# Decoder block on one Trainium2 core: the feed-forwards' output parts added to H by an accumulating transfer

## The chip, the cores and the metric

The kernel runs on one core of one Trainium2 chip. The core has a matrix engine (TensorE, PE in the profile; PEld is its weight load), VectorE (DVE), ScalarE (ACT), GpSimd (POOL), a queue engine (SyncE, SP) that issues transfers, and 16 DMA engines that carry them. Each engine works through its own instructions in the order in which the program gave them; an instruction that waits holds up everything behind it on its engine. The metric is the device time of one execution in microseconds. Before the change two runs gave 990.43 and 991.58 us, a median of 991.0 us.

## What is computed

One decoder block on 512 tokens of width 1024, in float32. Two SwiGLU feed-forwards stand around a token mixer, each with its own normalisation, shift, scale and gate; the modulation comes from a condition vector `c`.

```python
def swiglu(u, w_in, w_out):
    a, b = jnp.split(u @ w_in, 2, axis=-1)
    return (jax.nn.silu(a) * b) @ w_out
...
        u = modulate(rmsnorm(h, g_norm_ffn1[l]), sh1, sc1)
        h = h + 0.5 * gt1 * swiglu(u, w_ffn1_in[l], w_ffn1_out[l])
        u = modulate(rmsnorm(h, g_norm_mix[l]), sh2, sc2)
        h = h + gt2 * token_mixing(u, cos, sin, w_in[l], w_pool[l], pool_scale[l],
                                   w_pool_branch[l], w_attn_branch[l], w_out[l])
        u = modulate(rmsnorm(h, g_norm_ffn2[l]), sh3, sc3)
        h = h + 0.5 * gt3 * swiglu(u, w_ffn2_in[l], w_ffn2_out[l])
    return rmsnorm(h, g_final)
```

The hidden width of each feed-forward is 2816. The change touches the two lines `h = h + 0.5 * gt * swiglu(...)`, and of them only how the sum over the hidden width is added to `h`.

## The kernel before

**Layout.** Everything is held feature-major: `H` is eight tiles `H[0]` to `H[7]` of 128 features by 512 tokens in float32, 256 KB each, and stays in on-chip memory throughout. Every product is done in three matmuls (`mm3`, lines 360 to 362): the weights and the activations are each split into a high and a low part of a shorter format, and high times high, high times low and low times high are summed in one bank of the matrix engine's accumulator memory. There are eight banks of 128 x 512; the feed-forwards go round six of them (`nb`).

**Weights.** They arrive from main memory in chunks, mostly 512 KB (128 x 1024), by transfers of the SP queue (`fetch`, line 245). `split_hi` (ScalarE, line 317) copies a chunk into the ring `whi`, and `split_lo` (VectorE, line 329) subtracts to get `wlo`. `look(4)` makes sure that the splits of the next four chunks are in the program ahead of the matmuls that come now. Some chunks are not loaded as such but made by VectorE from two others (`make`, line 261), as the products of the hidden layer are done in a seven-product scheme in place of eight.

**One feed-forward.** The 22 tiles of the hidden width are made in pairs: the first few by `ffn_pair`, the others by `duo`, which runs seven `product`s of 24 matmuls of 256 columns each (lines 745 to 747) into three banks A, B and C. After product 0, ScalarE copies A to C; product 2 goes on adding to A, and so cannot begin before that copy is done. The output product is cut into five parts of the hidden width, `PARTS = ((0, 4), (4, 8), (8, 12), (12, 16), (16, 22))`. As soon as four hidden tiles are ready, a part runs: for each of the eight output tiles `m`, two by two, 12 matmuls of 512 columns into a bank, and then line 900, one VectorE instruction that multiplies the bank by the gate and adds it to `H[m]`. In the first pair of a part the matmuls of the two banks are interleaved. The first four parts go this way, in both feed-forwards: 2 x 4 x 8 = 64 instructions of line 900. The fifth part has another code (line 933 and `out_tail` or `out_end`), since the next normalisation starts beside it, and is not touched. Between two parts lie more pairs of the hidden layer, so each of the first four parts is followed by at least one `duo`.

**What else runs there.** In the first feed-forward VectorE also multiplies the modulation weights (`bg`, `ada_do`, line 387): a 512 KB row block of `w_ada`, loaded by SP into `cs`, `AR` or another buffer, once for each output tile in parts 1 to 3. Actions that a `duo` puts off (`later`) come at `step()`.

**Order.** The tile framework is told to keep the program's order on each engine (`manual_schedule`) and puts in the semaphores: an instruction that writes a tile waits for the last reader of what lay there before. A tile of a pool with `bufs=1`, such as those of `fw`, has one place, and each new tile of the same name takes it again.

Of the kernel before, what the change touches and what calls it, by code (L numbers as in the profile page):

```python
# [8 lines left out]
F32 = mybir.dt.float32  # L9
F32R = mybir.dt.float32r  # L10
I32 = mybir.dt.int32
AF = mybir.ActivationFunctionType
OP = mybir.AluOpType

P = 128
T = 512
# [117 lines left out]
def pairs_before(n, part):  # L134

    k1 = PARTS[part][1]
    return k1 if part + 1 == len(PARTS) or (n == 2 and part == 0) else k1 + 2
# [9 lines left out]
class Kernel:  # L147
# [6 lines left out]
    def plan(self):  # L154
# [38 lines left out]
        def ffn(n, ins, outs, first):  # L193
# [4 lines left out]
            for part, (k0, k1) in enumerate(PARTS):  # L198
# [9 lines left out]
                plain(outs[part * KT // 2:(part + 1) * KT // 2] if part + 1 < len(PARTS) else outs[-KT:])  # L208

        ffn(0, f1i, f1o, FIRST)  # L210
        shift(4)
        base = len(self.order)
# [5 lines left out]
        self.shifted.update(range(base, base + 4))  # L218
        shift(3)
        ffn(2, f2i, f2o, 0)  # L220
        shift(5)
        self.fetched = self.done = self.made = 0
# [638 lines left out]
    def ffn(self, n, j, last=None):  # L861

        nc, v = self.nc, self.nc.vector
        gate = self.mod[:, 24 * n + 16:24 * n + 24]

        def beside():
            if n == 0:
                self.bg()
                if part == 0:
                    self.bg()  # L870

        for part, (k0, k1) in enumerate(PARTS):
            tail = part + 1 == len(PARTS)
            extra = 1
            while j < pairs_before(n, part):
                if j < PLAIN[n]:
                    self.ffn_pair(j, beside)
                    j += 1
                else:
                    self.duo(n, j, last, tail and j + 2 == FT, extra)  # L880
                    last, extra = None, 0
                    j += 2
            if n == 0:
                last = self.beside_out(part) or last
            nk = k1 - k0
            hk = [(self.HH[k % NH], self.HL[k % NH]) for k in range(k0, k1)]
            if not tail:
                for m in range(0, KT, 2):
                    self.look(4)
                    w = self.take()  # L890
                    bs = [self.nb(), self.nb()]

                    for ka, kb in ((0, nk - 1), (nk - 1, nk)) if m == 0 else ():
                        for i in range(2):
                            for k in range(ka, kb):
                                self.mm3(bs[i], *w[nk * i + k], *hk[k], k == 0, k == nk - 1)
                    for i, b in enumerate(bs):
                        for k in range(nk if m else 0):
                            self.mm3(b, *w[nk * i + k], *hk[k], k == 0, k == nk - 1)
                        v.scalar_tensor_tensor(self.H[m + i], b, gate[:, m + i:m + i + 1], self.H[m + i],  # L900
                                               op0=OP.mult, op1=OP.add)

                        if n == 0 and part:
                            self.later((6, 13)[i], self.bg) if m + 2 == KT else self.bg()
                        if self.todo:
                            self.todo.pop(0)()
                    self.step()
                continue

            def ks(m):  # L910
                w = self.take()
                self.split_hi()
                return [(hi, lo, *hk[k]) for k, (hi, lo) in enumerate(w)]

            self.look()
            if n == 2:
                self.sums.close()
                op = self.f2.enter_context(self.tc.tile_pool(name="f2o", bufs=1))
                self.OO = op.tile([P, KT * T], F32, name="out").rearrange("p (m t) -> p m t", m=KT)
                self.O = [self.OO[:, m, :] for m in range(KT)]  # L920

            kl = [ks(0), ks(1)]
            bs = [self.nb(), self.nb()]
            for ka, kb in ((0, nk - 2), (nk - 2, nk)):
                for m in range(2):
                    for k in range(ka, kb):
                        self.mm3(bs[m], *kl[m][k], k == 0, k == nk - 1)
            for m in range(3 if n else 4):
                if m > 1:
                    bs.append(self.nb())  # L930
                    for k, x in enumerate(ks(m)):
                        self.mm3(bs[m], *x, k == 0, k == nk - 1)
                v.scalar_tensor_tensor(self.H[m], bs[m], gate[:, m:m + 1], self.H[m], op0=OP.mult, op1=OP.add)
                add = self.sumsq(m, self.H[m])
                if n == 2:
                    nc.scalar.activation(self.O[m], self.H[m], AF.Copy, scale=self.g(3)[:, m:m + 1])
                self.split_lo()
                add()
                if m:
                    self.split(self.done)  # L940
                self.fetch()
            if n:
                self.out_end((3, 4, 5, 6, 7), ks, gate)
            else:
                self.out_tail((4, 5, 6, 7), ks, gate, 1, lambda m: self.X[0][:, m % 2 * HT:])
# [849 lines left out]
```

## Time and profile before

| | |
|---|---|
| time of the two runs, us | 990.43 and 991.58, median 991.0 |
| span of the profiled execution, us | 988.9 |
| median of the runs less this span, us | 2.1 |
| mean granted TensorE clock | 0.999 |
| HBM read, written | 135.29 MB, 2.24 MB |
| first and last start of line 900, us from the start of the span | 92.8 and 908.1 |
| first and last start of line 933 (fifth parts), us | 327.7 and 958.5 |

The page has no time of the profiled execution besides its span, which runs from the first to the last instruction; the 2.1 us are what lies around it. Busy times are shares of that span. Matmuls overlap one another in the records (one is listed with 0.39 us although the next starts 0.23 us later), so the time of a row of matmuls is read from starts. Idle time of an engine that holds nobody up costs nothing.

### The profile page before, as it was taken

How to read it: one execution, taken by the hardware profiler on the slowest of the kernel's cores; microseconds unless marked ns; L12 is line 12 of the kernel's file. 1: busy time of each engine (PE TensorE's matmuls, PEld its weight loads, DVE VectorE, ACT ScalarE, POOL GpSimd, SP SyncE). 2: the span in 40 equal slices, each digit the busy share in tenths (PEclk: the TensorE clock that was granted, in tenths of full speed). 3: DMA queues.
4: the chain of work that ended last, by engine and by line, in shares of the span. 5: the costliest groups of instructions: out<-in, count | busy, mean ns of one | idle time of the engine just before them, and what ended most of it. 6: DMA issues, size and time to landing. Idle time of an engine off the chain costs nothing.

```text
span 988.9 us, 16359 instructions
## 1 busy us (share of the span) xinstructions
PE 980.7 (99%) x6688; PEld 893.3 (90%) x6688; DVE 784.3 (79%) x1090; ACT 474.7 (48%) x712; POOL 29.7 (3%) x31
## 2 busy tenths in 40 slices
PE   9999999999999999999999999999999999999997
PEld 7888999989999899888879998998899898998997
DVE  7989979889797777887878877868787776676764
ACT  5453643625435453445545552455355254352553
POOL 0000000000000000007200000000000000000002
PEclk9999999999999999999999999999999999999999
DMA  9856446465563426664233326513344134241312
GB/s 353 276 196 224 150 149 187 156 196 165 183 199 109 137 57 201 223 192 153 72 122 108 107 81 218 171 44 104 98 155 133 46 117 138 86 150 44 106 44 86
DMA packets 44876, 141.74 MB, mean 143 GB/s; under 512 B 6273, under 2 KB 9089, under 8 KB 44802
## 3 DMA queue, kind: packets, MB, share of 16 engines
q1 hardware_dynamic: 44224, 140.18, 43.9%
q8 instruction: 52, 0.85, 0.4%
q10 hardware_dynamic: 578, 0.53, 0.2%
q14 instruction: 22, 0.18, 0.1%
HBM read 135.29 MB, written 2.24 MB: 139 GB/s over the span
## 4 chain that ended last, share of the span: by engine, by line
PE 94%; DVE 2%; ACT 1%; SPq 1%; issue 1%; POOL 0%; DMA 0%; POOLq 0%; ACTq 0%; DVEq 0%
PE bank L360 15%; PE bank L361 15%; PE bank L362 15%; PE bank L746 13%; PE bank L745 13%; PE bank L747 13%; PE bank L1721 2%; PE bank L1723 1%; PE bank L1725 1%; SPq L1053 1%; PE bank L1397 1%; PE bank L1099 1%; PE bank L1150 1%; PE bank L1398 1%; PE bank L1399 1%
## 5 line engine op out<-in xcount | busy, mean ns | idle before, releaser
L329 DVE TENSOR_TENSOR wlo<-raw,whi 128x1024 fp32r<-128x1024 f32 (+4 forms) x162 | 170.6, 1066 | 52.2 <-ACT whi L317 51.9
L745 PE MATMUL bank<-UH,whi 128*128 128x256 f32 x640 | 176.7, 276 | 0.0
L746 PE MATMUL bank<-UL,whi 128*128 128x256 f32 x640 | 176.7, 276 | 0.0
L747 PE MATMUL bank<-UH,wlo 128*128 128x256 f32 x640 | 176.7, 276 | 0.0
L317 ACT ACTIVATE whi<-raw 128x1024 fp32r<-128x1024 f32 (+4 forms) x162 | 146.3, 920 | 58.4 <-DVE raw L261 55.0
L360 PE MATMUL bank<-HI,whi 128*128 128x512 f32 (+1 forms) x406 | 146.2, 360 | 0.0
L361 PE MATMUL bank<-HK,whi 128*128 128x512 f32 (+1 forms) x406 | 145.9, 359 | 0.0
L362 PE MATMUL bank<-HI,wlo 128*128 128x512 f32 (+1 forms) x406 | 145.8, 359 | 0.0
L329 DVE TENSOR_TENSOR wlo<-X,whi 128x1024 fp32r<-128x1024 f32 (+3 forms) x104 | 112.0, 1084 | 31.2 <-ACT whi L317 30.9
L745 PEld LDWEIGHTS bank<-UH,whi 128*128 128x128 f32 x640 | 120.1, 188 | 0.4
L746 PEld LDWEIGHTS bank<-UL,whi 128*128 128x128 f32 x640 | 120.2, 188 | 0.0
L747 PEld LDWEIGHTS bank<-UH,wlo 128*128 128x128 f32 x640 | 120.1, 188 | 0.0
L745 PE MATMUL bank<-SH,whi 128*128 128x256 f32 x408 | 112.7, 276 | 0.0
L746 PE MATMUL bank<-SL,whi 128*128 128x256 f32 x408 | 112.6, 276 | 0.0
L747 PE MATMUL bank<-SH,wlo 128*128 128x256 f32 x408 | 112.6, 276 | 0.0
L317 ACT ACTIVATE whi<-X 128x1024 fp32r<-128x1024 f32 (+3 forms) x104 | 95.7, 943 | 34.1 <-DVE X L261 33.4
L360 PE MATMUL bank<-UH,whi 128*128 128x512 f32 (+1 forms) x304 | 105.9, 348 | 0.0
L361 PE MATMUL bank<-UL,whi 128*128 128x512 f32 (+1 forms) x304 | 104.5, 344 | 0.1
L362 PE MATMUL bank<-UH,wlo 128*128 128x512 f32 (+1 forms) x304 | 104.2, 343 | 0.0
L362 PEld LDWEIGHTS bank<-HI,wlo 128*128 128x128 f32 x406 | 76.2, 188 | 11.7
L360 PEld LDWEIGHTS bank<-HI,whi 128*128 128x128 f32 x406 | 76.2, 188 | 11.5
L361 PEld LDWEIGHTS bank<-HK,whi 128*128 128x128 f32 x406 | 76.3, 188 | 11.3
(345 smaller groups left out, 1838.0 us busy)
## 6 DMA issues: line engine op xcount, KB each, us to landing
raw<-wmix SPq DMA_DIRECT2D x44, 512.0 KB, 3.8
raw<-wf1i SPq DMA_DIRECT2D x31, 512.0 KB, 4.7
raw<-wf2i SPq DMA_DIRECT2D x30, 512.0 KB, 3.7
ada<-wada SPq DMA_DIRECT2D x23, 512.0 KB, 5.6
AR<-wada SPq DMA_DIRECT2D x19, 512.0 KB, 4.5
X<-wf2i SPq DMA_DIRECT2D x14, 512.0 KB, 3.8
cs<-wada SPq DMA_DIRECT2D x12, 512.0 KB, 3.7
X<-wf1i SPq DMA_DIRECT2D x12, 512.0 KB, 4.3
```

Of the source, the lines that this page charges most:

```text
L317: self.nc.scalar.activation(self.hi[:, y], r[:, x], AF.Copy)
L329: self.nc.vector.tensor_tensor(self.lo[:, y], r[:, x], self.hi[:, y], op=OP.subtract)
L360: M(ps, hi, uh, start=start, stop=False)
L361: M(ps, hi, ul, start=False, stop=False)
L362: M(ps, lo, uh, start=False, stop=stop)
L745: M(o, hi, uh, start=start and p == 0 and k == 0, stop=False, skip_group_check=True)
L746: M(o, hi, ul, start=False, stop=False, skip_group_check=True)
L747: M(o, lo, uh, start=False, stop=k == 3, skip_group_check=True)
L1053: nc.sync.dma_start(w[32 * o:32 * o + 32], t[32 * i:32 * i + 32])
L1099: nc.tensor.matmul(S[:, o], q[:, toks], k[:, ks], start=True, stop=True, skip_group_check=True)
L1150: self.nc.tensor.matmul(self.bO[64 * h:64 * h + 64, P * hp:P * hp + P], x, pt[:, (2 * h + j) * P:(2 * h + j + 1) * P], start=j == first, s ...
L1721: M(b, hi, self.UH[k], start=k == 0, stop=False)
```

## The change

In the first four output parts of both feed-forwards, the VectorE instruction of line 900 is gone. In its place ScalarE copies the bank, times the gate (one number for each of the 128 partitions), to a tile `add0` or `add1`, for the even and the odd output tile of a pair; and a transfer that GpSimd issues reads this tile and adds it to `H[m]` where `H[m]` lies. Both tiles belong to the pool `fw`, which has one place for each name, so the copy for output tile `m + 2` waits until the transfer of output tile `m` is over. `fw` grows by these two tiles of 2 KB in each partition, and the pools that are opened after it lie 4 KB further on.

```diff
-                        v.scalar_tensor_tensor(self.H[m + i], b, gate[:, m + i:m + i + 1], self.H[m + i],
-                                               op0=OP.mult, op1=OP.add)
+                        t = self.fw.tile([P, T], F32, name=f"add{i}")
+                        nc.scalar.activation(t, b, AF.Copy, scale=gate[:, m + i:m + i + 1])
+                        nc.gpsimd.dma_start(self.H[m + i], t, accum_op=OP.add)
```

## The prediction

> **What bounds the kernel now.** I read the page first: the busy times, the chain of work that ended last, and the DMA queues.
>
> ```profile
> span 988.9 us, 16359 instructions
> PE 980.7 (99%) x6688; PEld 893.3 (90%) x6688; DVE 784.3 (79%) x1090; ACT 474.7 (48%) x712; POOL 29.7 (3%) x31
> ...
> q1 hardware_dynamic: 44224, 140.18, 43.9%
> ...
> PE 94%; DVE 2%; ACT 1%; SPq 1%; issue 1%; POOL 0%; DMA 0%; POOLq 0%; ACTq 0%; DVEq 0%
> ```
>
> The matrix engine is idle for 988.9 - 980.7 = 8.2 us in all, and 94% of the chain is its own work. VectorE, which the change relieves, has 2% of the chain. Next, the busy times by stretch, for the output parts that line 900 belongs to (three of the eight, and the sum over all eight; columns: length, PE, PEld, DVE, ACT, POOL with their counts, granted clock, DMA share, GB/s).
>
> ```profile
> 80.50:102.30 21.80, 21.80 (x97) 18.02 (x97) 20.48 (x28) 9.19 (x12) 0.00 (x0) 1.00 0.58 199
> ...
> 201.80:223.60 21.80, 21.80 (x102) 18.22 (x101) 19.16 (x31) 4.64 (x5) 0.00 (x0) 1.00 0.55 175
> ...
> 827.00:849.00 22.00, 22.00 (x103) 18.40 (x102) 15.20 (x19) 6.01 (x7) 0.00 (x0) 1.00 0.14 47
> ...
> sum 175.20, PE 175.20 PEld 146.69 DVE 138.82 ACT 48.41 POOL 0.00; mean PE 21.90 PEld 18.34 DVE 17.35 ACT 6.05 POOL 0.00
> ```
>
> PE is busy for 175.20 of 175.20 us: where the change acts there is no idle matrix time to win. So the question is only whether the new route holds the matmuls up. Last, the timeline of one part and the start of the `duo` behind it, on three engines.
>
> ```profile
> 826.08 0.40 PE L360 MATMUL bank<-HI,whi 128*128 128x512 f32 x1
> ...
> 847.87 0.27 PE L366 MATMUL bank<-UH,whi 128*128 128x240 f32 x1
> 847.98 0.28 PE L745 MATMUL bank<-UH,whi 128*128 128x256 f32 x1
> ...
> 850.71 0.28 PE L745 MATMUL bank<-SH,whi 128*128 128x256 f32 x1
> ```
>
> ```profile
> 831.07 1.43 DVE L900 SCALAR_TENSOR_TENSOR H<-bank,mod,H 128x512 f32<-128x512 f32 x2 [1.98 <-PE bank L362]
> ...
> 837.19 0.75 DVE L900 SCALAR_TENSOR_TENSOR H<-bank,mod,H 128x512 f32<-128x512 f32 x1 [0.56 <-PE bank L362]
> ...
> 842.63 0.75 DVE L900 SCALAR_TENSOR_TENSOR H<-bank,mod,H 128x512 f32<-128x512 f32 x1 [1.76 <-PE bank L362]
> ...
> 848.07 0.75 DVE L900 SCALAR_TENSOR_TENSOR H<-bank,mod,H 128x512 f32<-128x512 f32 x1 [1.76 <-PE bank L362]
> ```
>
> ```profile
> 850.91 0.58 ACT L752 ACTIVATE bank<-bank 128x512 f32<-128x512 f32 x1 [5.22 <-PE bank L747]
> 851.40 1.05 ACT L317 ACTIVATE whi<-raw 128x1024 fp32r<-128x1024 f32 x1
> ```
>
> A part's 96 matmuls take 847.87 - 826.08 = 21.79 us without a hole, a bank of 12 is ready every 2.72 us, a pair every 5.44 us (837.19, 842.63, 848.07). Line 900 waits for PE each time, nobody for it. Product 0 of the `duo` starts at 847.98, product 1 at 850.71, so product 2 at 850.71 + 2.73 = 853.44; it needs ScalarE's copy of A to C, which runs 850.91 to 851.49. That is the first deadline that ScalarE meets behind a part.
>
> **What is taken off VectorE.** The costs of both routes, from the groups of instructions:
>
> ```profile
> L900 DVE SCALAR_TENSOR_TENSOR H<-bank,mod,H 128x512 f32<-128x512 f32 x64 | 47.2, 749 | 28.1 <-PE bank L362 28.1
> L1050 ACT ACTIVATE rt<-bank,cst 128x512 f32<-128x512 f32 x4 | 2.8, 689 | 5.7 <-PE bank L362 5.7
> L745 PE MATMUL bank<-UH,whi 128*128 128x256 f32 x640 | 176.7, 276 | 0.0
> L745 PE MATMUL bank<-SH,whi 128*128 128x256 f32 x408 | 112.7, 276 | 0.0
> ```
>
> 64 x 0.749 us, 47.2 us with the overlaps, and 28.1 us of waits ahead of them leave VectorE. It lets the splits and `make`s behind them start earlier, and on the path that is worth nothing, because PE waits for none of them: 0 us.
>
> **What is put on ScalarE.** 64 copies from a bank with a factor for each partition. Line 1050 is the same shape and form: 0.69 us. A part has eight, 5.5 us; ScalarE has 4.6 to 9.2 us of work in the 21.8 us, so it stays below 15. As work this is hidden. What can hurt is the order: a copy that waits holds the splits and `duo` copies behind it. It waits for two things. The bank, as line 900 did: the splits behind it then come no earlier than the pair that is being multiplied, and they are four chunks ahead of need, one chunk a pair, so 0. And the place of its tile, held until the transfer of two output tiles earlier is over.
>
> **The tile's turn.** Call c the time from one copy's start to the end of its transfer. The copy of tile m1 starts at 837.19 - 5.44 = 831.75 in that part. Three turns later comes m7, so it starts at the later of 848.07 and 831.75 + 3c; the even tiles start 0.7 us earlier with the same c, and give the same bound. Behind m7 stand 0.69 us of itself, one split (1.05) and the copy of A to C (0.58), to be over at 853.44. So m7 may start up to 851.12, and c up to (851.12 - 831.75) / 3 = 6.46 us costs nothing. Beyond it PE stands 3c - 19.4 us in a part, 24c - 155 us in eight. Banks come round after three pairs and are no tighter.
>
> The trace has no transfer issued by GpSimd and none that adds. The nearest rows (DMA issues with KB and median us to landing; then SP's issue times, ns least, median, most):
>
> ```profile
> k<-wada SPq DMA_DIRECT2D x6, 512.0 KB, 6.3
> ...
> rt<-tr SPq DMA_DIRECT2D x16, 64.0 KB, 2.0
> ...
> out_dram<-out SPq DMA_DIRECT2D x4, 256.0 KB, 2.2
> tr<-wmix SPq DMA_DIRECT2D x3, 256.0 KB, 4.0
> ```
>
> ```profile
> L245 SPq DMA_DIRECT2D X<-wf2i x14: 327/328/672, 692.7 to 910.0; - x14
> ...
> L1053 SPq DMA_DIRECT2D rt<-tr x16: 512/582/590, 398.3 to 440.8; - x16
> ```
>
> Least: 0.33 us issue and 2.2 us landing, c = 0.69 + 0.33 + 2.2 = 3.2. Most: 0.58 and 6.3 (512 KB among other loads, since the addition reads 256 KB from each of two places), c = 7.6. I take 0.58 and 4.0, the 256 KB load that came down among others: c = 5.3. Then m2, due only 3.4 us after m0, waits 1.9 us and m6 some 1.6 us; m7 starts on time. Cost 0; at the upper end (24 x 7.6) - 155 = 27 us.
>
> **What is put on the DMA engines.** 64 x 262,144 bytes = 16.8 MB, or 33.6 MB if the read of H counts as much. At q1's rate (43.9% for 140.18 MB) that is 5 to 11% more. It is tightest in the first feed-forward: 175 GB/s at a share of 0.55 makes 318 GB/s at full share, and a part's 2.1 MB or 4.2 MB need 6.6 or 13.2 us of 21.8: 0.85, or 1.16 and 3.4 us of backlog. That delays a weight load or a `w_ada` load for VectorE, which after the change has 21.8 - (19.16 - 6.0) = 8.6 us free there; the splits are two to four chunks (5 us and more) ahead. Cost 0; without that cover 3.4 x 4 = 14 us.
>
> **What is put on GpSimd.** Its busy time in the parts is 0.00, so no work of it is delayed; it waits for each copy, with only the next addition behind it. H is next read late:
>
> ```profile
> L933 DVE SCALAR_TENSOR_TENSOR H<-bank,mod,H x7: 745/750/751, 327.7 to 958.5; 128x512 f32<-128x512 f32 x7
> ```
>
> Line 933 first runs at 327.7, two `duo`s behind the fourth part. The 4 KB by which later pools move: the matmul is 276 ns from UH as from SH, which lie apart, so 0.
>
> **One rule against the change.** GpSimd's work beside VectorE is seen in the mixer:
>
> ```profile
> 440.90 1.22 DVE L329 TENSOR_TENSOR wlo<-raw,whi 128x1024 fp32r<-128x1024 f32 x1
> ...
> 452.17 2.08 DVE L329 TENSOR_TENSOR wlo<-raw,whi 128x1024 fp32r<-128x1024 f32 x1
> ```
>
> ```profile
> 451.27 1.90 POOL L1223 TENSOR_TENSOR rt<-tr 128x527 f32<-128x527 f32 x1 [8.03 <-ACT tr L1217]
> ```
>
> The same subtraction takes 0.86 us longer beside a GpSimd addition. If each of 64 issues did this, VectorE would lose 55 us, against 47 us taken off: still no wait of PE. The Trainium skill ("SBUF — State Buffer", Who interferes with whom) says that an instruction of VectorE with two inputs in this memory contends with a GpSimd instruction that reads it, which the two rows bear out, and not with one that only writes; by it the writing of descriptors would cost VectorE nothing, and the sum is the same. Its box on VectorE keeping GpSimd from writing descriptors is the third rival below.
>
> **The rivals.** First, *the tile's turn is too long* (slower): c above 6.46, from the issue or from a landing like the 6.3 us row. At c = 7.6 it is 991 + 27 = 1018 us; 2% (20 us) begins at c = 7.3. For it: the 512 KB rows and a doubled read; against it: the 2.0 and 2.2 us of on-chip reads, and a DMA share of 0.14 in the second feed-forward. Second, *the addition goes piece by piece* (slower): if the 256 KB landed as four 64 KB rows one after the other, 4 x 2.0, c = 0.69 + 0.58 + 8.0 = 9.3, and 24 x 9.3 - 155 = 68 us: 1059. No row speaks for or against it. Third, *VectorE holds GpSimd up* (slower): were each issue to wait for two of VectorE's 1.22 us instructions, c = 5.3 + 2.4 = 7.7 and the time 991 + 30 = 1021. VectorE is busy 15 to 20 of 22 us there, which is for it; 8 issues in 21.8 us leave room, which is against it. The Trainium skill ("SBUF — State Buffer", SBUF: two separate sides) gives that blocking for modes in which VectorE uses both port pairs, and names copies; nearly all instructions in these parts have two tensors, so it should be rare here. Fourth, *VectorE's share of the chain shrinks* (faster): 2 us of the 8.2 us of idle PE, 989; the chain's VectorE pieces lie at the ends of stages, where line 900 isn't. Fifth, *it does not do what it says*, VectorE still waiting for the additions before its next use of H: that use is two `duo`s later, so 991 again.
>
> **How the numbers follow.** 988.9 span, 2.1 around it by the median, 0 of change: 991. Chances: forecast 0.57, tile's turn 0.21, piece by piece 0.09, VectorE holds GpSimd 0.07, faster 0.04, fifth 0.02. Below 988 lies at most 0.02. Above: 0.09 of the second rival and perhaps 0.08 of the first and third beyond 1030 (24 x 8.1 - 155 = 39 us); the range 988 to 1030 so holds about 0.8. The forecast case alone is 988 to 996. About 2% is what a measurement can tell from no change. Slower by more: 0.09 and all but 0.03 of 0.28, 0.34. Faster by more would need 20 us where PE idles 8.2: 0.01. Within: 0.65.
>
> **What the changed profile would show.** Right: PE busy without holes in the eight parts and the `duo`s behind them, DVE down by about 47 us, ACT up by about 44 us (64 x 0.69), the copies waiting under 2 us for their tiles, 4 to 5 us from issue to landing. Wrong: ScalarE's copy waiting for DMA by more than 3 us at m7, holes in PE after product 1 of the first `duo`, in the first feed-forward more than the second if the loads do it, in both alike if it is the addition itself; subtractions of 2 us if GpSimd contends.

## The result and the profile after

The changed kernel takes 1017.24 us, the median of two runs (1016.83 and 1017.64), against 991.0 before: a ratio of 1.0271, 95% interval 1.0254 to 1.0288. It is slower by 26 us, where no change that could be measured was forecast. The page of the profiled execution, whose own time was 1017.64 us (busy times; queues with packets, MB and share; the chain by engine; the group of line 901; the transfer's row with KB and median us from the start of its issue to landing):

```profile
span 1015.7 us, 16560 instructions
PE 991.4 (98%) x6688; PEld 903.1 (89%) x6688; DVE 743.8 (73%) x1026; ACT 514.6 (51%) x776; POOL 85.7 (8%) x95
...
q1 hardware_dynamic: 44224, 140.18, 42.7%
q0 software_dynamic: 9216, 16.78, 9.5%
...
PE 66%; issue 26%; POOL 3%; DVE 2%; DMA 2%; SPq 1%; ACT 1%; POOLq 0%; ACTq 0%; DVEq 0%
...
L901 ACT ACTIVATE add<-bank,mod 128x512 f32<-128x512 f32 x64 | 43.7, 688 | 107.7 <-DMA H<-add 70.5
...
H<-add POOLq DMA_DIRECT2D x64, 256.0 KB, 3.9
```

The engines' work moved as planned: VectorE has 40.5 us less, ScalarE 39.9 us more, one copy takes 688 ns. But ScalarE's copies now wait 70.5 us in all for an addition, and the matrix engine, idle for 8.2 us before, is idle for 1015.7 - 991.4 = 24.3 us.

Where the 26.8 us of span came from is read from one matmul that every part has, line 366 behind the end of the part, taken from the timelines of both kernels. From one such point to the next the changed kernel needs 6.67, 5.91, 6.79 and 7.12 us more over the four intervals that begin at the ends of parts 0 to 3 of the first feed-forward, 26.5 us together. From there to the end it loses nothing more (its lag goes from 27.0 to 26.4 us). So the whole loss lies in the first feed-forward, behind its four parts. One of them, part 1, on ScalarE (start, duration, operation, and in brackets how long ScalarE stood idle before it and what ended that):

```profile
152.85 1.37 ACT L901 ACTIVATE add<-bank,mod 128x512 f32<-128x512 f32 x2 [3.24 <-PE bank L362]
...
159.76 0.69 ACT L901 ACTIVATE add<-bank,mod 128x512 f32<-128x512 f32 x1 [4.51 <-DMA H<-add]
...
168.00 0.69 ACT L901 ACTIVATE add<-bank,mod 128x512 f32<-128x512 f32 x1 [3.23 <-DMA H<-add]
...
174.86 0.69 ACT L901 ACTIVATE add<-bank,mod 128x512 f32<-128x512 f32 x1 [3.99 <-DMA H<-add]
176.12 0.69 ACT L901 ACTIVATE add<-bank,mod 128x512 f32<-128x512 f32 x1 [0.57 <-DMA H<-add]
176.71 1.05 ACT L317 ACTIVATE whi<-X 128x1024 fp32r<-128x1024 f32 x1
177.66 0.59 ACT L752 ACTIVATE bank<-bank 128x512 f32<-128x512 f32 x1
```

The copy of m0 starts at 152.85, that of m1 0.68 us behind it, at 153.53. The even tiles' place comes round at 159.76, 168.00 and 174.86: turns of 6.91, 8.24 and 6.86 us. The last copy, m7, starts at 176.12, and right behind it stand one split and the copy of A to C, exactly the queue of the prediction. On the matrix engine in the same place:

```profile
175.10 0.28 PE L747 MATMUL bank<-SH,wlo 128*128 128x256 f32 x1
178.29 0.58 PE L745 MATMUL bank<-SH,whi 128*128 128x256 f32 x1 [2.92 <-ACT bank L752]
178.67 0.42 PE L746 MATMUL bank<-SL,whi 128*128 128x256 f32 x1
178.89 0.42 PE L747 MATMUL bank<-SH,wlo 128*128 128x256 f32 x1
```

Product 1 ends, product 2 waits for C, and no matmul starts for 178.29 - 175.10 = 3.19 us, 3.08 us beyond the spacing of 0.11. Then a second loss is seen: the matmuls that follow start 0.22 us apart, not 0.11. The busy times by stretch show why (length, PE, PEld, DVE, ACT, POOL, granted clock, DMA share, GB/s; part 1 itself, the hole, and what follows):

```profile
146.90:168.70 21.80, 21.80 (x102) 18.23 (x102) 16.21 (x23) 7.92 (x11) 3.50 (x4) 1.00 0.81 213
...
175.20:178.20 3.00, 0.17 (x2) 0.00 (x0) 0.41 (x1) 2.43 (x5) 1.73 (x2) 0.99 0.31 55
178.20:182.00 3.80, 3.71 (x19) 3.71 (x20) 3.80 (x4) 2.56 (x4) 0.00 (x0) 0.56 1.01 220
182.00:186.00 4.00, 4.00 (x37) 4.00 (x36) 3.27 (x4) 1.79 (x3) 0.00 (x0) 1.00 0.76 273
```

During the part PE is busy throughout. Behind the hole the granted clock is 0.56 over 3.8 us, in which 19 matmuls run, against 37 in the 4 us at full clock that follow. The four holes are 5.37, 3.08, 3.91 and 4.23 us, 16.6 together; the other 26.5 - 16.6 = 9.9 us, 1.3 to 2.9 us a hole, lie in slower matmuls behind them. The half clock is not all of it. Behind parts 1 and 2 the matmuls then start 0.1178 us apart for some 30 us, up to the next part, where the same instructions of the kernel without any addition (it comes at the end of the experiments) start 0.1133 us apart. The first row is of the changed kernel, the second of that one:

```profile
186.00:212.00 26.00, 26.00 (x224) 26.00 (x222) 20.93 (x25) 15.15 (x21) 0.00 (x0) 1.00 0.43 139
```

```profile
174.00:200.00 26.00, 26.00 (x232) 26.00 (x231) 21.84 (x26) 15.40 (x21) 0.00 (x0) 1.00 0.43 140
```

The granted clock and the DMA engines' share are the same, and eight matmuls fewer run in 26 us: 1.2 us are lost so behind each of these two parts, and the remaining 7.5 us by the half clock behind all four. Why the spacing stays wider after a stop is not shown.

What stood in front of the additions is on SP's queue (the issues of that stretch), with GpSimd's between them:

```profile
152.04 0.33 SPq L379 DMA_DIRECT2D cs<-wada  x1
153.18 0.33 SPq L379 DMA_DIRECT2D AR<-wada  x1
157.80 0.33 SPq L379 DMA_DIRECT2D cs<-wada  x1
159.65 0.33 SPq L379 DMA_DIRECT2D AR<-wada  x1
```

```profile
153.94 1.76 POOL L902 DMA_DIRECT2D H<-add  x2 [40.39 <-ACT add L901]
```

Two `w_ada` blocks of 512 KB are issued in the 2 us ahead of the first two additions, and two more ahead of the next. In the second feed-forward, where no `w_ada` is loaded, the same code looks like this on ScalarE:

```profile
857.48 1.37 ACT L901 ACTIVATE add<-bank,mod 128x512 f32<-128x512 f32 x2 [3.24 <-PE bank L362]
...
861.98 0.69 ACT L901 ACTIVATE add<-bank,mod 128x512 f32<-128x512 f32 x1 [2.09 <-DMA H<-add]
...
866.48 0.69 ACT L901 ACTIVATE add<-bank,mod 128x512 f32<-128x512 f32 x1 [0.25 <-DMA H<-add]
...
874.52 0.69 ACT L901 ACTIVATE add<-bank,mod 128x512 f32<-128x512 f32 x1 [2.03 <-PE bank L362]
```

Two turns of 4.50 us, and m7 waits for the matrix engine, not for a transfer: no hole. Three of the four parts there run so. The first does not:

```profile
726.81 0.69 ACT L901 ACTIVATE add<-bank,mod 128x512 f32<-128x512 f32 x1 [4.34 <-DMA H<-add]
```

The copy of its m0 starts at 718.83, so this turn is 7.98 us. SP issues five 512 KB weight loads between 714 and 722, and no `w_ada`. The later turns are short, m7 starts at 738.21, and as the part ends at 735.26, it is only 0.30 us ahead of holding PE up.

The prediction's equation can be tried on every part: PE stands if m7 starts more than 3.25 us behind the end of the part (851.12 - 847.87 there). Starts are from the timelines; c is a third of the time from m1 to m7, a mean of three turns.

| part of the first feed-forward | m1 starts | end of part | m7 starts | c | m7 late by | hole in PE |
|---|---|---|---|---|---|---|
| 0 | 92.95 | 102.81 | 111.57 | 6.2 | 5.51 | 5.37 |
| 1 | 153.53 | 169.65 | 176.12 | 7.5 | 3.22 | 3.08 |
| 2 | 219.43 | 235.55 | 242.77 | 7.8 | 3.97 | 3.91 |
| 3 | 286.21 | 302.33 | 309.95 | 7.9 | 4.37 | 4.23 |

Lateness and hole agree within 0.15 us in all four. Parts 1 to 3 have the free c of the prediction, (169.65 + 3.25 - 153.53) / 3 = 6.46, and exceed it. Part 0 doesn't: its m1 starts late, and its free c is only (102.81 + 3.25 - 92.95) / 3 = 4.4.

### The profile page after: what moved, and what is told of

The parts are those of the page before. It is cut to its first block, busy times and chain, and to the rows that moved or that the text cites. A ratio compares the mean times of both kernels' runs of the same rounds, so it can differ in the third digit from the quotient of the medians.

```text
span 1015.7 us, 16560 instructions
## 1 busy us (share of the span) xinstructions
PE 991.4 (98%) x6688; PEld 903.1 (89%) x6688; DVE 743.8 (73%) x1026; ACT 514.6 (51%) x776; POOL 85.7 (8%) x95
## 3 DMA queue, kind: packets, MB, share of 16 engines
q0 software_dynamic: 9216, 16.78, 9.5%
## 4 chain that ended last, share of the span: by engine, by line
PE 66%; issue 26%; POOL 3%; DVE 2%; DMA 2%; SPq 1%; ACT 1%; POOLq 0%; ACTq 0%; DVEq 0%
PE bank L360 11%; PE bank L362 11%; PE bank L361 11%; PE bank L745 9%; PE bank L746 9%; PE bank L747 9%; POOL H L902 2%; DMA H<-add 1%; SPq L1054 1%; PE bank L1398 1%; PE bank L1100 1%; PE bank L1151 1%; PE bank L1399 1%; PE bank L1400 1%; PE bank L1133 1%
## 5 line engine op out<-in xcount | busy, mean ns | idle before, releaser
L317 ACT ACTIVATE whi<-raw 128x1024 fp32r<-128x1024 f32 (+4 forms) x162 | 146.1, 920 | 12.3 <-DVE raw L261 9.8
L745 PE MATMUL bank<-SH,whi 128*128 128x256 f32 x408 | 116.6, 286 | 15.9 <-ACT bank L752 15.9
L746 PE MATMUL bank<-SL,whi 128*128 128x256 f32 x408 | 115.9, 284 | 0.0
L747 PE MATMUL bank<-SH,wlo 128*128 128x256 f32 x408 | 115.9, 284 | 0.0
L902 POOL DMA_DIRECT2D H<-add x64 | 56.0, 901 | 688.2 <-ACT add L901 681.6
L901 ACT ACTIVATE add<-bank,mod 128x512 f32<-128x512 f32 x64 | 43.7, 688 | 107.7 <-DMA H<-add 70.5
L745 PEld LDWEIGHTS bank<-SH,whi 128*128 128x128 f32 x408 | 79.6, 195 | 16.7 <-ACT bank L752 16.7
```

The source lines that it names most:

```text
L317: self.nc.scalar.activation(self.hi[:, y], r[:, x], AF.Copy)
L745: M(o, hi, uh, start=start and p == 0 and k == 0, stop=False, skip_group_check=True)
L746: M(o, hi, ul, start=False, stop=False, skip_group_check=True)
L747: M(o, lo, uh, start=False, stop=k == 3, skip_group_check=True)
L901: nc.scalar.activation(t, b, AF.Copy, scale=gate[:, m + i:m + i + 1])
L902: nc.gpsimd.dma_start(self.H[m + i], t, accum_op=OP.add)
```

## The experiments

The theory going in: in the first feed-forward the additions queue behind SP's loads, the tile's place comes free too late, and ScalarE's waiting copy holds up the copy of A to C. The rivals: the addition itself is too slow everywhere; the added traffic delays the loads and so the matmuls; the half clock comes from the DMA traffic and not from the hole. All edits are against the changed kernel, and ratios against the kernel before on the same chip.

### Which feed-forward

```diff
-                        t = self.fw.tile([P, T], F32, name=f"add{i}")
...
+                        if n == 0:
+                            t = self.fw.tile([P, T], F32, name=f"add{i}")
...
+                        else:
+                            v.scalar_tensor_tensor(self.H[m + i], b, gate[:, m + i:m + i + 1], self.H[m + i],
+                                                   op0=OP.mult, op1=OP.add)
```

> The new route only in the first feed-forward, VectorE's old instruction in the second. Theory (a tile's turn is over 6.46 us only where w_ada loads share the DMA engines): all of the loss is here, 1017 us, with holes of 3 to 5 us in PE behind each of its four parts. Rival (the addition by transfer is slow by itself, in both feed-forwards): about half of the loss, 1004 us.

Measured 1011.85 us, ratio 1.0216 (1.019 to 1.0242); holes of 4.17, 2.11, 2.17 and 2.81 us. With `if n == 2` in place of `n == 0`:

> The new route only in the second feed-forward, where no w_ada is loaded. Theory: turns of 4.5 us as in the changed kernel, no hole, 990 to 992 us. Rival (the addition is slow by itself): about half of the loss, 1004 us.

Measured 990.88 us, ratio 1.0003 (0.9994 to 1.0012), no hole. The second feed-forward's share of the change costs nothing and brings nothing. The first one's alone costs 21 us, 5 to 6 less than the whole change, although its instructions are the same up to the end of the first feed-forward. The four runs spread from 1008.85 to 1015.51. The profiled one is the fastest, 8.8 us below the changed kernel's: its four holes are 5.3 us shorter together, and by the clock records of the two traces it spends 10.2 us at half clock behind them, not 17.1, which is worth about 3 us more. Why the landings behind the loads were shorter in this kernel stays open.

### The wait alone: four places

```diff
-                        t = self.fw.tile([P, T], F32, name=f"add{i}")
+                        t = self.fw.tile([P, T], F32, name=("u2", "u3", "add0", "add1")[(m + i) % 4])
```

The tiles turn over four places (`u2` and `u3` are tiles that `fw` has already); every copy, issue, transfer and byte stays.

> The copies go round four tiles (two of them those of u2 and u3, idle in these parts), everything else as in the changed kernel. Theory (ScalarE waits for the tile's place): a copy waits for the transfer of four output tiles earlier, 10.9 us, so turns of 7 to 8 us cost nothing: 991 us, no hole. Rival (the additions take the DMA engines from the weight loads, or GpSimd's issues slow VectorE): the traffic and the issues are the same, so it stays at 1010 us or more.

Measured 991.36 us, ratio 1.0008 (0.9999 to 1.0017), and again with more runs:

> The changed kernel with four tiles again, in five rounds, as the candidate for a version that keeps VectorE free and loses nothing. Theory: the same as the kernel before and as the one without any addition, within 0.15%, as the traffic costs nothing once nobody waits for it. Rival (the 16.8 MB of transfers take from the weight loads): 0.3% slower or more, 994 us.

991.33 us, 1.0007 (0.9998 to 1.0015). One stretch with a part of the first feed-forward in it, by engine, and one of ScalarE's copies:

```profile
140.00:172.00 32.00, 32.00 (x189) 28.23 (x188) 23.97 (x30) 14.99 (x20) 6.97 (x8) 1.00 0.91 238
```

```profile
153.57 0.69 ACT L901 ACTIVATE add<-bank,mod 128x512 f32<-128x512 f32 x1 [2.03 <-PE bank L362]
```

The copies wait for the matrix engine, as line 900 did; PE is busy for 32.00 of 32.00 us. The DMA engines have a share of 0.91, more than in the slow kernel's part 1 (0.81), and a landing still takes 4.5 us by the median. So the traffic as such costs nothing beyond the 0.2% that the intervals leave open: only the wait for the place does. The rival of delayed loads falls.

### What the turns wait behind: the loads

```diff
-        for c in np.split(np.arange(D), n):
+        for c in np.split(np.arange(64 if 26 <= j < 48 else D), n):
```

The `w_ada` loads beside parts 1 to 3 keep their number and shrink from 512 to 32 KB.

> The changed kernel with 22 of the w_ada loads of the first feed-forward's parts cut from 1024 columns to 64; VectorE still multiplies all 1024 columns, the others holding older data, so the mixer's modulation is not computed rightly. Theory (these loads lengthen the turn): turns in the first feed-forward fall from 7 to 8 us to under 5.5 us, no hole, 991 us. Rival (the order of the work in the first feed-forward does it, not the traffic): turns over 6.5 us remain, 1010 us or more.

Measured 999.75 us, ratio 1.0084 (1.0064 to 1.0105). Part 1 on ScalarE:

```profile
153.46 1.37 ACT L901 ACTIVATE add<-bank,mod 128x512 f32<-128x512 f32 x2 [3.24 <-PE bank L362]
157.94 0.69 ACT L901 ACTIVATE add<-bank,mod 128x512 f32<-128x512 f32 x1 [2.08 <-DMA H<-add]
```

The first turn is 157.94 - 153.46 = 4.48 us, that of the second feed-forward. The later ones in the part are 4.5 to 6.9 us (a 512 KB weight load is still issued among them, at 159.98), so that the "under 5.5" expected holds for some only; c, by the table's measure, is 5.9, 5.7 and 5.9 us in parts 1 to 3, under the free 6.46, and the holes behind these parts are gone. The 991 us expected were missed, because the hole behind part 0 stays, at 5.85 us, with 1.8 us of slow matmuls: part 0 lies ahead of those loads. Another 2.3 us are lost in the second feed-forward, where m7 of the first part comes 0.28 us late this time: no half clock follows, but from 722 to 776 the matmuls start 0.1178 us apart, not 0.1133. What comes down beside part 0 of the first feed-forward are weights. So these were cut too, first alone:

```diff
-            for c in self.pieces(i, w):
+            for c in self.pieces(i, 64 if name == "wf1i" and 16 <= i < 24 else w):
```

> The changed kernel with eight weight loads of the first feed-forward, those that come down during and right behind its first output part, cut to 64 columns, so that these products are made with older data. Theory (the loads beside the additions lengthen the turn, whatever they carry): the hole behind the first part, 5.4 to 5.8 us with some 2 us of slow clock, goes and the other three stay: 1008 to 1011 us. Rival (the first part's hole has another cause): 1017 us.

Measured 1013.11 us, ratio 1.0231 (1.0204 to 1.0258). The hole behind part 0 shrinks to 2.07 us, the others stay at 3.76, 3.90 and 3.69. Both edits together:

> Both cuts together, the w_ada loads and these eight weight loads. Theory: no hole in the first feed-forward, 991 to 993 us. Rival (something besides the loads makes the turn long there): a hole of 3 us or more is left, 996 us or more.

Measured 995.64 us, ratio 1.005 (1.0036 to 1.0063): only part 0's hole is left, 2.12 us. The loads that are cut take away the hole of the part that they lie beside, or most of it for part 0, and no other; the expected times were missed by what remains of part 0's.

### What remains of part 0

In the profile of the kernel with both loads cut, ScalarE stands idle at the start of part 0, waiting for VectorE, and then has splits and the hidden layer's S copies to do before the first copies of the part:

```profile
89.32 0.63 ACT L675 ACTIVATE HI<-u 128x512 fp32r<-128x512 f32 x1 [6.55 <-DVE u L673]
91.75 0.67 ACT L901 ACTIVATE add<-bank,mod 128x512 f32<-128x512 f32 x1
93.28 0.67 ACT L901 ACTIVATE add<-bank,mod 128x512 f32<-128x512 f32 x1
...
108.52 0.69 ACT L901 ACTIVATE add<-bank,mod 128x512 f32<-128x512 f32 x1 [0.81 <-DMA H<-add]
```

One thought was that the S copies between the first turns stretch them, by their place in ScalarE's order. They were put ahead of the part, with both loads cut and without that:

```diff
                 last = self.beside_out(part) or last
+                if part == 0:
+                    for _ in range(3):
+                        self.todo.pop(0)()
+                    self.todo[:0] = [lambda: None] * 3
```

> The kernel with both cuts of the loads, and the three splits of S (ScalarE's copies and VectorE's subtractions, which stood between the first copies of the first part) moved ahead of that part. Theory (the 2.1 us hole that was left comes from the order: a copy that waits for its tile holds the third S copy, that holds VectorE's make, that holds the split and with it the next copy): no hole, 991 to 992 us. Rival (the first part's turns are long for another reason): the hole stays, 995 to 996 us.

Measured 998.9 us, ratio 1.0081 (1.0066 to 1.0096); the hole grew to 4.23 us.

> The changed kernel with only the three S splits moved ahead of the first part, all loads whole. Theory (order and loads both make the first part's hole): the hole of 5.4 to 5.8 us shrinks, the other three stay: 1011 to 1015 us. Rival (the loads alone make it): 1017 us.

Measured 1018.01 us, ratio 1.0282 (1.0259 to 1.0305); the first hole is 5.48 us and three small ones of 0.62 to 0.95 us appear ahead of it. The thought was wrong. What the part's own numbers show is the equation again. With both loads cut, m1 starts at 93.28 and m7 at 108.52, turns of 5.1 us, which the free 6.46 would carry; but the part ends at 103.01, so m7 is due by 106.26 and comes 2.26 us late, for a hole of 2.12. With the S copies ahead, the first copy starts at 93.65, 5.3 us behind that copy to HI (88.36 in this profile) and not 2.4; the part ends at 102.14, m7 starts at 109.75 and is 4.36 us late, for a hole of 4.23. So the edit made the start later still. It is the late start that leaves part 0 with a free c of 4.4 us in place of 6.46.

### The length of the turn, and the number of places

One place in place of two, everything else the same:

```diff
-                        t = self.fw.tile([P, T], F32, name=f"add{i}")
+                        t = self.fw.tile([P, T], F32, name="add")
```

> The changed kernel with one tile for all copies. Theory: seven turns in a row stand between m0 and m7, each 4.5 us in the second feed-forward and 5.5 to 7 us in the first. Holes of 831.07 + 7 x 4.5 - 851.12 = 11.5 us and of 18.5 to 29 us in a part, with some 2 us of slow clock behind each: 1120 to 1170 us. Rival (it isn't the wait for the place): 1017 us.

Measured 1142.02 us, ratio 1.1522 (1.1485 to 1.156). A part of the second feed-forward on ScalarE, and PE behind it:

```profile
876.27 0.69 ACT L901 ACTIVATE add<-bank,mod 128x512 f32<-128x512 f32 x1 [3.24 <-PE bank L362]
...
907.83 0.69 ACT L901 ACTIVATE add<-bank,mod 128x512 f32<-128x512 f32 x1 [3.80 <-DMA H<-add]
```

```profile
898.52 0.28 PE L747 MATMUL bank<-SH,wlo 128*128 128x256 f32 x1
910.00 0.58 PE L745 MATMUL bank<-SH,whi 128*128 128x256 f32 x1 [11.21 <-ACT bank L752]
```

From m0 to m7 are now seven turns, (907.83 - 876.27) / 7 = 4.51 us each, where the two places have three. The holes of the second feed-forward are 15.24, 11.37, 11.24 and 11.95 us, for 11.5 expected; the longest is that of its first part, whose first turn, behind the weight loads, is 8.3 us. Those of the first feed-forward are 12.73 to 20.29, for 18.5 to 29 expected. So the second feed-forward was free by its two places alone, not because its transfers were hidden as such. With three places in place of two:

```diff
-                        t = self.fw.tile([P, T], F32, name=f"add{i}")
+                        t = self.fw.tile([P, T], F32, name=("u2", "add0", "add1")[(m + i) % 3])
```

> Three tiles in place of two (u2 as the third). A copy waits for the transfer of three output tiles earlier, 8.2 us. Theory (only the turn against the spacing counts): turns of 7 to 8 us just fit, 991 to 994 us. Rival (the additions' traffic itself delays the matmuls' weights once they come faster): 1000 us or more.

Measured 993.05 us, ratio 1.0024 (1.0015 to 1.0033), as expected: the only hole is 0.78 us, behind part 0. From one place to four the time goes 1142.0, 1017 to 1018, 993.1, 991.3.

### What the adding costs

```diff
-                        nc.gpsimd.dma_start(self.H[m + i], t, accum_op=OP.add)
+                        nc.gpsimd.dma_start(self.H[m + i], t)
```

> The changed kernel with the transfer writing the tile over H in place of adding it, so the residual is left out. Theory (the turn is long because 256 KB wait among 512 KB loads): a little shorter, without the read of H, 1005 to 1015 us. Rival (the adding is what takes long): no hole, 991 us.

Measured 995.89 us, ratio 1.0045 (1.0027 to 1.0063), between the two expectations; the holes are 1.28, 0.68, 1.13 and 1.82 us. The changed kernel first, then this one (issue times in ns, least, median, most; the transfers' us from the start of the issue to landing):

```profile
L902 POOL DMA_DIRECT2D H<-add x64: 852/872/1202, 92.4 to 935.6; - x64
...
DMA to landing us min/median/max: 3.2/3.9/9.1
```

```profile
L902 POOL DMA_DIRECT2D H<-add x64: 538/538/708, 92.8 to 915.9; - x64
...
DMA to landing us min/median/max: 2.2/2.3/7.1
```

And the plain transfers' queue on its page:

```profile
q0 software_dynamic: 5120, 16.78, 4.4%
```

The same 16.78 MB as a plain transfer lands 1.0 us earlier at the least, of which 0.33 us are the shorter issue: 1.0 us a turn and 3 us a part of three turns, which is most of a hole; and it takes 4.4% of the DMA engines' time, not 9.5%, in 5120 packets, not 9216. Both the queued loads and the slower addition are needed for the holes behind parts 1 to 3: without the `w_ada` loads c is 5.7 to 5.9 us, under 6.46, and with plain transfers behind them 6.7 to 7.1, just above.

### The half clock

The changed kernel once more, beside one that fills the hole: 28 matmuls of 256 columns into a bank that nobody reads, ahead of product 2 of the first `duo` behind each of the four parts.

```diff
+            if i == 2 and n == 0 and extra:
+                for _ in range(28):
+                    nc.tensor.matmul(self.B[7][:, :HT], self.UH[5][:, :P], self.UH[4][:, :HT], start=True, stop=True,
+                                     skip_group_check=True)
```

> The changed kernel as it is, beside the next three on one chip: 1017 us, holes in PE of 3 to 5.4 us behind the four parts of the first feed-forward only, and a granted clock near 0.55 in the 3 us after each.

> The changed kernel with 28 matmuls of 256 columns, that nobody reads, ahead of product 2 of the first duo behind each part of the first feed-forward: 3.2 us of PE work in place of standing still. Theory (a stall costs twice: the hole, and then a lower granted clock because PE stood): the holes shrink by 3.2 us, the time of the extra matmuls, so nothing is lost by them, and the slow matmuls behind the holes, 7 to 10 us in all, mostly go: 1008 to 1011 us. Rival (the matmuls behind a hole are slow because the DMA engines are full then): 1017 us.

The changed kernel measured 1018.01 us, ratio 1.0274 (1.0251 to 1.0297), as before; the filled one 1012.14, ratio 1.0218 (1.0194 to 1.0243). The hole behind part 0 and the 3.3 us that follow it, from the busy times by stretch, in the changed kernel and then in the filled one:

```profile
109.00:115.10 6.10, 0.51 (x5) 0.31 (x3) 1.72 (x2) 3.99 (x7) 2.60 (x3) 0.88 0.51 89
115.10:118.40 3.30, 3.29 (x15) 3.29 (x16) 3.07 (x4) 2.46 (x4) 0.00 (x0) 0.50 0.88 228
```

```profile
108.60:113.20 4.60, 3.41 (x29) 3.20 (x27) 1.40 (x2) 2.83 (x5) 1.74 (x2) 1.00 0.66 114
113.20:116.50 3.30, 3.26 (x28) 3.27 (x29) 3.07 (x4) 2.71 (x5) 0.00 (x0) 1.00 0.78 176
```

Behind the empty hole 15 matmuls run in 3.3 us at a clock of 0.50; behind the filled one 28, at 1.00, with the DMA engines nearly as busy (0.78 for 0.88; in the kernel with four places the clock was 1.00 at a share of 0.91). It is the idle time, not the traffic, that halves the clock. The saving of about 6 us fell just short of what was expected. The 28 added matmuls take 3.4 us, which behind parts 1 and 2 is longer than the wait was; holes of 1.40 and 1.69 us are left behind parts 0 and 3; and the wider spacing of 0.1178 us still follows parts 1 and 2.

### What could have been won

Copy and transfer taken out, so that neither VectorE nor ScalarE nor GpSimd has anything of line 900:

> The changed kernel without copy and transfer: the first four output parts of both feed-forwards are multiplied, but never added to H. Nothing of line 900 is left on any engine. Theory (VectorE's old instruction held nobody up): 989.5 to 991.5 us, as before. Rival (VectorE's 47 us were partly on the path, and the changed kernel loses more than it shows): 988 us or less.

Measured 990.67 us, ratio 1.0001 (0.9992 to 1.001). Relieving VectorE of all 64 instructions, with nothing put in their place, is worth nothing. No version of this change can beat the kernel before by more than the 0.1% that this interval leaves open.

## Why the prediction was wrong

**What held.** The matrix engine was the bound and nothing could be won: shown by the kernel without the additions. The copy cost 0.688 us for 0.69. The tile's turn was the right thing to watch, m7 with one split and the copy of A to C behind it the right deadline, and the equation, with each part's own start and end, right within 0.15 us where a hole formed. Three of the four parts of the second feed-forward ran as the forecast case said, and the first got by with 0.30 us to spare. The DMA engines' added share, 9.5%, lay in the 5 to 11% named. The sign in the changed profile that was to mean "wrong because of the loads", holes in the first feed-forward more than in the second, is what came. The stated range of 988 to 1030 us holds the measured time, but only by the room made for rivals: the forecast case alone was 988 to 996.

**The step that failed** is "I take 0.58 and 4.0, the 256 KB load that came down among others: c = 5.3 ... Cost 0", used for all eight parts. One landing stood for two stages whose DMA engines are loaded quite differently, 0.55 to 0.58 against 0.14 in the prediction's own rows. In three parts of the second feed-forward the turn is 4.5 us; in the first feed-forward c is 6.2 to 7.9, the upper end named there (7.6, from 512 KB among other loads). Cutting the `w_ada` loads brought c to 5.7 to 5.9 in parts 1 to 3, and the holes behind them went. It is not the feed-forward as such that decides: beside five weight loads c is 6.3 us in the second one's first part too.

**The same omission in the DMA step.** A backlog of 3.4 us a part was worked out, and then asked only whether it delays a load: "Cost 0". It wasn't asked whether the additions wait behind the loads. They are the transfers with someone waiting: 6.46 us free against the loads' 5 us and more of chunks ahead. By c = 5.3 + 3.4 = 8.7 the slower rival would have been the forecast for the first feed-forward.

**Two terms mis-sized.** GpSimd's issue took 0.87 us for 0.58; the least landing of an addition is 3.2 us, between the 2.2 and 4.0 of the rows chosen, and 1.0 above a plain transfer's. The sum for c also counts the issue twice, since the view's time to landing runs from the start of the issue: in the second feed-forward a copy starts at 857.48, its issue at 858.57, 0.40 us after the copy's end, and 3.28 us later the transfer has landed, 4.4 us in all; 0.69, 0.87 and 3.28 added up would be 4.8, more than the turn of 4.50 that was measured. The sum leaves out the 0.40 us between copy and issue, so by luck the two errors nearly cancel, and 5.3 is above 4.5 mainly because the landing taken was 4.0 us and not 3.3.

**Two terms missing.** The start of m1 was taken from a part of the second feed-forward. In part 0 of the first it comes 6 us and more later in the part, and this stood in the trace of before: the first line 900 ran at 92.8 in a stretch that starts at 80.50, 12.3 us in, against 831.07 - 826.08 = 5.0 us in the part that was used. And the sum counted a hole at its length; the slower matmuls behind it added 9.9 to 16.6 us of holes. The Trainium skill ("TensorE: Matmul & The Clock Gate", The HAM clock gate) says that the matrix engine's clock falls to half after an idle window of about 3.4 us and rises again after about as long under load; the changed kernel's trace agrees for its holes, of 3.08 us and more, with 0.50 for 3.4 or 6.8 us at a time by its clock record, and in the filled kernel holes of 1.40 and 1.69 us were followed by full clock. Holes between 2.0 and 2.7 us went either way, which is shown below.

**The rivals.** The first is the one that came, at its place and near its time, 1018, but by other terms: it reckoned eight parts with 3.4 us each, and there were four with some 6.6, of which 4.1 are hole and 2.5 the slower matmuls behind it. The time agreeing is in part chance. The second falls: four pieces one after the other would take 8.0 us, and additions land in 3.2 at the least. The third falls too: half of GpSimd's issues took 852 to 872 ns and the longest 1202, far from 2.4 us on top of each, and VectorE's subtraction shows no trace of them, 1230 ns by the mean of 109 in both kernels:

```profile
L329 DVE TENSOR_TENSOR wlo<-raw,whi 128x1024 fp32r<-128x1024 f32 x109 | 133.9, 1230 | 71.4 <-ACT whi L317 71.4
```

The fourth falls by the kernel without the additions, 990.67 us, and the fifth too: no instruction of VectorE waits for an addition in the changed profile.

**What stays open.** Why the holes were shorter when only the first feed-forward was changed. And why matmuls that have once stopped start 0.1178 us apart up to the next part behind some parts and not behind others, at the same granted clock.

## What to carry to other kernels

A tile with few places, written by a compute engine and read by a transfer, puts that transfer's landing into the engine's own order: compare the turn of a place with the time between its uses, stage by stage, with the landing that large loads issued just ahead would give in that very stage. Then follow the queue behind the waiting instruction to the next deadline of the bound engine, from the latest start of any such stage and not a typical one. And where the bound engine is full, relieving another is worth nothing, so every wait that the relief brings is pure risk.

## What was not expected of the hardware

An addition by a transfer of 256 KB in float32 within on-chip memory took 2.2 times the DMA engines' time of a plain one (9.5% of the span's 1015.7 us against 4.4% of 995.9), 1.8 times the packets, 0.87 us for 0.54 to issue, and 1.0 us more from the start of the issue to landing. The Trainium skill ("DMA: Bandwidth & Descriptors", Anatomy of one DMA) gives a GpSimd-issued transfer 2.0 us and its bytes at 436 GB/s, an estimate of 2.6 us here; the plain one, with 2.3 us from the start of the issue to landing by the median, is close to that, the adding one, with 3.3 us in the second feed-forward, is 0.7 us above. And a hole of 3 to 5 us in the matrix engine cost 1.3 to 2.9 us more behind it.

How short a hole must be to leave the clock full depends on where it lies. The trace keeps the start of every change of the granted clock, and within a profile the stretches at 0.50 start on a grid of 3.41 us: at 113.27, 178.12, 246.39 and 311.24 in the changed kernel, 19, 20 and 19 steps apart. In the kernel with only the first feed-forward changed, the holes behind parts 1 and 2 are 2.11 and 2.17 us long and end at 176.78 and 240.68. The steps in which they end and those behind (busy times by stretch):

```profile
174.87:178.28 3.41, 1.50 (x13) 1.50 (x14) 2.01 (x2) 3.31 (x5) 1.30 (x2) 1.00 0.73 125
178.28:181.69 3.41, 3.41 (x19) 3.41 (x18) 3.38 (x4) 1.72 (x3) 0.00 (x0) 0.50 0.97 241
```

```profile
239.71:243.12 3.41, 2.44 (x20) 2.44 (x21) 3.10 (x4) 3.19 (x5) 0.68 (x1) 1.00 1.08 169
243.12:246.53 3.41, 3.41 (x31) 3.41 (x30) 3.38 (x4) 1.79 (x3) 0.00 (x0) 1.00 0.91 311
```

Of the first hole 1.91 us fall into one step, and the next runs at 0.50. The second is cut in two by the grid, 1.21 and 0.96 us, and the clock stays full. Every hole behind a part that begins at full clock, in all profiles of the runs here, fits this: 1.91 us and more of one step were followed by 0.50, 1.87 us and less by full clock, a hole of 2.63 us in two pieces of 1.02 and 1.61 among them. By the page on the clock gate (the Trainium skill, "TensorE: Matmul & The Clock Gate", The HAM clock gate) the window of 3.4 us runs freely, so that where a hole lies in it matters, and the trace agrees; that 1.91 us of a window can be enough is not what the page states, and the first two rows show it.
